# Latent attention rebuilt with four heads side by side, inside a three-block transformer kernel

## The chip, the core and the metric

The program runs on one core of a Trainium2 chip. A core has five engines that run their own in-order streams of instructions and wait for one another through semaphores: PE (matrix multiplication), ACT, DVE, POOL and SP (which here only issues DMAs). The metric is the device time of one execution in microseconds, the median of several runs; lower is better. The profile comes from one execution of its own.

## The reference, cut to what matters

256 tokens of width 1024 go through three blocks: a mixer with a feed-forward net, latent attention with a feed-forward net, and a chunked attention with a gated net. All is float32. Only the latent attention in the middle is touched:

```python
C_HEADS, C_NOPE, C_ROPE, C_V, Q_LORA, KV_LORA = 16, 64, 32, 64, 384, 256

def mla_mixer(h, positions, w_in, q_g, kv_g, w_uq, w_ukv, w_out):
    cq, ckv, kr = jnp.split(h @ w_in, [Q_LORA, Q_LORA + KV_LORA], axis=-1)
    q = (rms_norm(cq, q_g) @ w_uq).reshape(bsz, seq, C_HEADS, C_NOPE + C_ROPE)
    kv = (rms_norm(ckv, kv_g) @ w_ukv).reshape(bsz, seq, C_HEADS, C_NOPE + C_V)
    ...
    q_rope = apply_rope(q[..., C_NOPE:], cos, sin)
    k_rope = apply_rope(kr[:, :, None, :], cos, sin)
    qf = jnp.concatenate([q[..., :C_NOPE], q_rope], axis=-1)
    kf = jnp.concatenate([kv[..., :C_NOPE], jnp.broadcast_to(k_rope, ...)], axis=-1)
    v = kv[..., C_NOPE:]
    ...
        s = jnp.einsum("bqhd,bkhd->bhqk", qblk, kf) * scale
        pr = jax.nn.softmax(s, axis=-1)
        return jnp.einsum("bhqk,bkhd->bqhd", pr, v)
    ...
    return o @ w_out
```

A head's score is thus a product over 96 numbers: 64 of its own ("nope") and 32 rotated ones ("rope"), whose key is the same for all 16 heads.

## The kernel before

Everything is kept feature by feature: a tile holds 128 features on its partitions and the 256 tokens along its rows. A weight matrix comes in chunks of 1 MB. `Stream` handles them: SP loads a chunk into `raw`, ACT rounds it to `whi`, and DVE (or POOL, for the chunks listed in `ON_POOL`) makes the rest `wlo = raw - whi`. `Stream.done()` puts these pieces into a list of due times (`later`), and each group of matmuls advances the clock of that list by `later.tick`. A chunk's splitting can begin when one of four pairs `whi`, `wlo` is free, that is when PE has finished with an older chunk. A product in nearly full precision takes three matmuls, `three`: high by high, high by low, low by high. In this document such a group of three, 256 columns each, is called a triple. Plain float32 matmuls (scores, transposes, values by probabilities) take two passes each in the trace, so one of them shows as two.

The stage of latent attention goes in this order. `tgemm` with `c_evac` makes the five latent tiles (40 triples), in the order keys first (2 tiles), queries (3 tiles), four of them side by side. `rkv_chain` and `rq_chain` work out the norms of the latents; `kv_split` multiplies the latent keys by their norm and only then splits them into `ch` and `cl`. `thin` makes the shared rotated key, which SP copies into all heads by a DMA (line 989). `uq_evac` and `uk_evac` bring queries and keys into `qT` and `kT`, 96 partitions by head, after 36 and 16 triples. Then the values, 24 matmuls of 512 columns (lines 1086 to 1088).

`attend(i)` runs the 16 heads one after another: `sc` the scores (line 1028), a maximum on DVE (1032), two exponentials on ACT (1035), `nrm` the division on DVE (1043), `tr` four transposes (1050) and a copy (1052), `pv` the product with the values (1062). The scores go to the PSUM pool `mm`, four banks; transposes and products go to `aux`, four banks too. The output projection (`tgemm` with `residual`, 64 triples) takes four tiles side by side, then the others in twos, with the last heads mixed in. The order of PE's instructions is chosen by a scheduler in this stage, as is that of the other engines. The feed-forward net follows at once: its first triples need `x` block by block.

## Time and profile before

| | us |
|---|---|
| median of 3 runs | 912.94 |
| lowest, highest | 912.53, 916.38 |
| the profiled execution, its own time | 918.1 |
| its span, first to last instruction | 916.4 |
| PE busy in the span | 889.9 (97%) |
| DVE, ACT, POOL busy | 583.3, 481.3, 268.0 |

The profiled execution lies 5.2 us above the median, so what is worked out from it is used as a difference and put on the median. PE is busy almost all the time: only work taken from PE, or one of its few waits, can shorten the whole. "Busy" counts a matmul that streams at half the clock as fully busy, so the granted clock has to be read beside it.

### The profile page before, as it was taken

The page shows a single profiled execution, that of the slowest core. Times are in us where ns is not written, and L with a number is a line of the kernel's source. Part 1 is how long each engine was busy: PE and PEld are TensorE (multiplying, and loading weights), DVE is VectorE, ACT ScalarE, POOL GpSimd, SP SyncE. Part 2 cuts the span into 40 slices and gives each one's busy share as a digit, 9 for nine tenths or more (in the row PEclk, how much of TensorE's full clock was granted, in tenths as well). Part 3 has the DMA queues.
Part 4 walks back from the last instruction along what each step waited for, and adds up shares of the span by engine and source line. Part 5 has one row for each costly group of instructions (what it writes and reads, how often), then busy time and mean ns, then how long its engine had stood idle before and what let it go on. Part 6 is the DMA issues. An engine that isn't in the chain of part 4 may idle for free.

```text
span 916.4 us, 16411 instructions
## 1 busy us (share of the span) xinstructions
PE 889.9 (97%) x6680; PEld 824.1 (90%) x6680; DVE 583.3 (64%) x943; ACT 481.3 (53%) x848; POOL 268.0 (29%) x269
## 2 busy tenths in 40 slices
PE   7899999999999998999999999999999999999997
PEld 5788999999999987679999999999967789999885
DVE  7697889555555379846755555547783766666442
ACT  6675467555444275756555544424376665544331
POOL 5876733333011266047333301110147000000000
PEclk9999999999999998999999999999999999999999
DMA  8543454655554336014565555549432465555521
GB/s 293 199 150 126 142 187 161 230 189 191 188 191 164 109 116 230 1 57 150 207 211 189 191 187 191 185 164 248 189 138 93 174 246 191 194 185 189 189 82 46
DMA packets 26107, 154.90 MB, mean 169 GB/s; under 512 B 2752, under 2 KB 5744, under 8 KB 8752
## 3 DMA queue, kind: packets, MB, share of 16 engines
q1 hardware_dynamic: 22704, 148.70, 45.6%
q10 hardware_dynamic: 3040, 4.36, 1.9%
q8 instruction: 52, 0.85, 0.4%
q0 software_dynamic: 288, 0.79, 0.3%
q14 instruction: 23, 0.19, 0.1%
HBM read 152.25 MB, written 1.07 MB: 167 GB/s over the span
## 4 chain that ended last, share of the span: by engine, by line
PE 58%; DVE 1%; issue 0%; ACT 0%; DVEq 0%; POOLq 0%; ACTq 0%
PE mm L368 12%; PE mm L369 12%; PE mm L370 12%; PE aux L466 2%; PE aux L465 2%; PE aux L467 2%; PE mm L1028 2%; PE aux L1062 2%; PE mm L430 2%; PE mm L432 2%; PE mm L431 2%; PE aux L1050 1%; PE mm L465 1%; PE mm L467 1%; PE mm L466 1%; PE aux L1219 1%
## 5 line engine op out<-in xcount | busy, mean ns | idle before, releaser
L149 ACT ACTIVATE whi<-raw 128x1024 fp32r<-128x1024 f32 (+3 forms) x318 | 284.9, 949 | 240.2 <-PE mm L369 157.0
L152 DVE TENSOR_TENSOR wlo<-raw,whi 128x1024 fp32r<-128x1024 f32 (+2 forms) x254 | 307.5, 1246 | 124.4 <-ACT whi L149 122.7
L368 PE MATMUL mm<-xh,whi 128*128 128x256 f32 x1072 | 301.4, 281 | 0.8 <-DVE head L494 0.8
L369 PE MATMUL mm<-xl,whi 128*128 128x256 f32 x1072 | 299.1, 279 | 0.0
L370 PE MATMUL mm<-xh,wlo 128*128 128x256 f32 x1072 | 299.0, 279 | 0.0
L370 PEld LDWEIGHTS mm<-xh,wlo 128*128 128x128 f32 x1072 | 203.9, 190 | 0.0
L368 PEld LDWEIGHTS mm<-xh,whi 128*128 128x128 f32 x1072 | 202.0, 188 | 1.7 <-DVE head L494 1.0
L369 PEld LDWEIGHTS mm<-xl,whi 128*128 128x128 f32 x1072 | 202.0, 188 | 0.2
L368 PE MATMUL mm<-hh,whi 128*128 128x256 f32 x512 | 143.9, 281 | 0.0
L369 PE MATMUL mm<-hl,whi 128*128 128x256 f32 x512 | 143.9, 281 | 0.0
L370 PE MATMUL mm<-hh,wlo 128*128 128x256 f32 x512 | 143.9, 281 | 0.0
L152 POOL TENSOR_TENSOR wlo<-raw,whi 128x512 fp32r<-128x512 f32 (+2 forms) x64 | 84.5, 1349 | 67.0 <-ACT whi L149 66.9
L370 PEld LDWEIGHTS mm<-hh,wlo 128*128 128x128 f32 x512 | 98.3, 192 | 0.0
L368 PEld LDWEIGHTS mm<-hh,whi 128*128 128x128 f32 x512 | 96.1, 188 | 0.0
L369 PEld LDWEIGHTS mm<-hl,whi 128*128 128x128 f32 x512 | 96.1, 188 | 0.0
L519 POOL TENSOR_TENSOR fu<-ft 128x512 f32<-128x512 f32 (+1 forms) x36 | 54.7, 1521 | 119.3 <-ACT ft L517 111.6
L313 POOL TENSOR_TENSOR s_acc<-s_acc,sq 128x256 f32<-128x256 f32 x37 | 43.9, 1193 | 155.2 <-ACT sq L312 144.6
L1120 POOL TENSOR_TENSOR r<-v,nhalf 128x1 f32<-128x1 f32 x4 | 2.2, 557 | 193.5 <-DVE v L1119 193.5
L430 PE MATMUL mm<-whi,xh 128*128 128x512 f32 x96 | 39.1, 424 | 1.9 <-ACT whi L149 1.9
L431 PE MATMUL mm<-wlo,xh 128*128 128x512 f32 x96 | 38.1, 400 | 2.2 <-DVE wlo L152 2.2
L520 DVE TENSOR_TENSOR hl<-fu,hh 128x512 fp32r<-128x512 f32 (+1 forms) x36 | 24.1, 675 | 23.4 <-POOL fu L519 23.4
L432 PE MATMUL mm<-whi,xl 128*128 128x512 f32 x96 | 37.9, 398 | 0.6 <-DVE xl L1329 0.6
(370 smaller groups left out, 1355.7 us busy)
## 6 DMA issues: line engine op xcount, KB each, us to landing
raw<-in_w_dram SPq DMA_DIRECT2D x64, 1024.0 KB, 4.8
raw<-in_w_gu_dram SPq DMA_DIRECT2D x22, 1024.0 KB, 4.8
raw<-in_w_qk_dram SPq DMA_DIRECT2D x12, 1024.0 KB, 6.1
raw<-in_w_down_dram SPq DMA_DIRECT2D x11, 1024.0 KB, 4.8
raw<-in_w_ab_out_dram SPq DMA_DIRECT2D x4, 1024.0 KB, 4.9
raw<-in_w_c_out_dram SPq DMA_DIRECT2D x4, 1024.0 KB, 4.8
raw<-in_w_v_dram SPq DMA_DIRECT2D x4, 1024.0 KB, 6.1
raw<-in_w_o_dram SPq DMA_DIRECT2D x4, 1024.0 KB, 4.9
```

Of the source, the lines that this page charges most:

```text
L149: self.nc.scalar.activation(hi[:, s], r[:, s], AF.Copy)
L152: eng.tensor_tensor(lo[:, s], r[:, s], hi[:, s].bitcast(F32), op=ALU.subtract)
L313: state["sum"] = (dve if k == last else pool).tensor_tensor(acc, acc, sq, op=ALU.add)
L368: pe.matmul(ps, wh, h, start=start, stop=False)
L369: pe.matmul(ps, wh, l, start=False, stop=False)
L370: pe.matmul(ps, wl, h, start=False, stop=stop)
L430: pe.matmul(pss[tt], h[k][:, ts], wh[:, s], start=k == 0, stop=False)
L431: pe.matmul(pss[tt], h[k][:, ts], wl[:, s], start=False, stop=False)
L432: pe.matmul(pss[tt], l[k][:, ts], wh[:, s], start=False, stop=k == nk - 1)
L465: pe.matmul(ps, h[k][:, ts], wh[:, ns], start=k == 0, stop=False)
L466: pe.matmul(ps, h[k][:, ts], wl[:, ns], start=False, stop=False)
L519: pool.tensor_tensor(u[:, 0:g], t[:, 0:g], t[:, 0:g], op=ALU.mult)
```

## The change

- The 16 heads are taken in four groups of four. The nope part of a score uses 64 rows of the PE array, two heads at a time on the two halves of the partitions. The rope part uses 32 rows, four heads at a time on the four quarters; it adds to the same PSUM banks. `qn`, `kn`, `qr` and `kr` hold these parts as the projections leave them, so the copies into 96 partitions by head are gone, and with them the DMA of the rotated key; `fold4` writes it to the four quarters.
- A pair's two products with the values (`pv`) alternate, each on 64 columns of the array.
- The latent keys are no longer multiplied by their norm before the split. `k_nope` and `values` apply it as they take their results from PSUM; `kv_split` goes.
- PE's order is now written out by hand over the whole stage (`manual_schedule`): the two latent tiles of the keys first, then the queries; the rope part, then nope queries and keys of one group ahead of the scores.
- The scores of a group take four `aux` banks, all there are; `tr` and `pv` take theirs from the same four.
- Half of the divisions in `nrm` move from DVE to POOL.
- The output projection goes `k` by `k` over all eight tiles in four `mm` banks, with one `pv` and one `tr` within each `k`.

```diff
-              "w_uq", "w_uk", "w_uv", "w_c_out", "w1_1", "w2_1", "w_qk2", "w_v2",
+              "w_uq", "w_uk", "w_uv", "w_uq2", "w_c_out", "w1_1", "w2_1", "w_qk2", "w_v2",
...
+    for i in range(4):
+        pool.tensor_copy(fold4[:, 32 * i:32 * i + 32], fold)
...
-        qT = ap.tile([96, NH, T], F32, name="qT")
-        kT = ap.tile([96, NH, T], F32, name="kT")
+        qn = [ap.tile([P, 2, T], F32, tag="q", name="qn", bufs=4) for _ in range(4)]
+        kn = [ap.tile([P, 2, T], F32, tag="k", name="kn", bufs=4) for _ in range(4)]
+        qr = ap.tile([P, 4, T], F32, name="qr")
+        kr = ap.tile([P, T], F32, name="kr")
         v = ap.tile([P, 2, D], F32, name="v")
-        yh = ap.tile([P, KB, T], F32R, name="yh")
...
-            bcast(rbc[1], rkv, dt=2.0)
-            later(2.1, kv_split)
-        def kv_split():
-            for j in range(2):
-                dve.tensor_tensor(ckv[:, j], ckv[:, j], rbc[1], op=ALU.mult)
-                act.activation(ch[:, j], ckv[:, j], AF.Copy)
-                dve.tensor_tensor(cl[:, j], ckv[:, j], ch[:, j].bitcast(F32), op=ALU.subtract)
+            bcast(rbc[1], rkv, dt=5.5)
...
-        later(3.3, c_chain)
-        tgemm(XH, XL, KB, 5, c_evac, lead=4, psums={4: auxt})
+            bcast(rbc[0], r_col[0], dt=5.0)
...
+        def tiles(w, b0, h, l, nk, n):
+            ps = mmt().rearrange("p (a b) -> p a b", a=2)
+            wh, wl = w
+            for i in range(n):
+                for k in range(nk):
+                    s = slice((b0 + i * nk + k) * P, (b0 + i * nk + k + 1) * P)
+                    three(ps[:, i], wh[:, s], wl[:, s], h[k], l[k], k == 0, k == nk - 1)
+            return ps
...
+        def q_rope(w, g):
+            ps = tiles(w, 6 * g, CK[2:5], CL[2:5], 3, 2)
+            qs = qr[:, 2 * g:2 * g + 2]
+            q2 = mp.tile([P, 2, T], F32, tag="q2", name="q2")
+            act.activation(qs, ps, AF.Copy)
+            for i in range(2):
+                dve.stream_shuffle(q2[:, i], qs[:, i], SHUF)
+                pool.tensor_tensor(qs[:, i], qs[:, i], cosT, op=ALU.mult)
+                dve.tensor_tensor(q2[:, i], q2[:, i], sinT, op=ALU.mult)
+                dve.tensor_tensor(qs[:, i], qs[:, i], q2[:, i], op=ALU.add)
+        def q_nope(w, g):
+            dve.tensor_copy(qn[g], tiles(w, 6 * (g % 2), CK[2:5], CL[2:5], 3, 2))
+        def k_nope(w, g):
+            ps = tiles(w, 4 * g, CK[0:2], CL[0:2], 2, 2)
+            for i in range(2):
+                dve.tensor_tensor(kn[g][:, i], ps[:, i], rbc[1], op=ALU.mult)
+        def values(w, n, tt):
+            ts = slice(tt * P, (tt + 1) * P)
+            ps = mmt()
+            wh, wl = w
+            for k in range(2):
+                s = slice(k * D + n * 512, k * D + n * 512 + 512)
+                pe.matmul(ps, ch[:, k, ts], wh[:, s], start=k == 0, stop=False)
+                pe.matmul(ps, ch[:, k, ts], wl[:, s], start=False, stop=False)
+                pe.matmul(ps, cl[:, k, ts], wh[:, s], start=False, stop=k == 1)
+            later.tick(1.3)
+            act.activation(v[:, tt, n * 512:(n + 1) * 512], ps, AF.Copy, scale=rkv[:, tt:tt + 1])
...
         kr4 = tmp.tile([P, T], F32, tag="rs", name="kr4")
+        mctx = tc.manual_schedule(engines={mybir.EngineType.PE})
+        mctx.__enter__()
+        later(4.2, c_chain)
...
+        w = S.get()
+        q_rope(w, 0)
+        key_rope()
+        q_rope(w, 1)
+        S.done()
+        w = S.get()
+        q_nope(w, 0)
+        wk = S.get()
+        k_nope(wk, 0)
+        q_nope(w, 1)
+        S.done(held=2)
+        k_nope(wk, 1)
+        wv = S.get()
+        values(wv, 0, 0)
...
-        nc.sync.dma_start(kT[64:96], spread(kr.unsqueeze(1), 1, NH))
...
+        def sc(a):
+            pss = [auxt().rearrange("p (a b) -> p a b", a=2) for _ in range(4)]
+            for p in range(2):
+                for qt in range(2):
+                    for i, rr in enumerate(HALF):
+                        pe.matmul(pss[2 * p + i][:, qt], qn[a][rr, p, qt * P:(qt + 1) * P], kn[a][rr, p],
+                                  start=qt == 0, stop=False)
             for qt in range(2):
+                for i in range(4):
+                    rr = slice(32 * i, 32 * i + 32)
+                    pe.matmul(pss[i][:, qt], qr[rr, a, qt * P:(qt + 1) * P], kr[rr], start=False, stop=qt == 1)
+            later.tick(2.6)
+            for p in range(2):
+                mx = mp.tile([P, 2, 2], F32, tag="mx", name="mx", bufs=3)
+                sm = mp.tile([P, 2, 2], F32, tag="sm", name="sm", bufs=8)
+                prs = [mp.tile([P, 2, T], F32, tag="pr", name="pr", bufs=16) for _ in range(2)]
+                for i in range(2):
+                    dve.tensor_reduce(mx[:, i], pss[2 * p + i], axis=AX, op=ALU.max)
+                dve.tensor_tensor(mx, mx, spread(nsrq.unsqueeze(1), 1, 2), op=ALU.mult)
+                for i in range(2):
+                    for qt in range(2):
+                        S.behind = act.activation(prs[i][:, qt], pss[2 * p + i][:, qt], AF.Exp,
+                                                  scale=srq[:, qt:qt + 1], bias=mx[:, i, qt:qt + 1],
+                                                  accum_out=sm[:, i, qt:qt + 1])
+                st_p[2 * a + p] = (prs, sm)
+        def nrm(j):
+            prs, sm = st_p[j]
             dve.reciprocal(sm, sm)
+            for i in range(2):
+                for qt in range(2):
+                    (pool if i else dve).tensor_scalar(prs[i][:, qt], prs[i][:, qt], sm[:, i, qt:qt + 1], None,
+                                                       op0=ALU.mult)
+        def tr(j):
+            prs, sm = st_p.pop(j)
+            st_t[j] = []
+            for i in range(2):
+                ps = auxt().rearrange("p (a b) -> p a b", a=2)
+                for kt in range(2):
+                    for qt in range(2):
+                        pe.transpose(ps[:, kt, qt * P:(qt + 1) * P], prs[i][:, qt, kt * P:(kt + 1) * P], ident)
+                pT = pT_[(2 * j + i) % 3]
+                (act.activation(pT, ps, AF.Copy) if i else dve.tensor_copy(pT, ps))
+                st_t[j].append(pT)
+            later.tick(0.9)
+        def pv(j):
+            pTs = st_t.pop(j)
+            o = auxt()
             for kt in range(2):
+                for i, rr in enumerate(HALF):
+                    pe.matmul(o[rr, 0:T], v[:, kt, (2 * j + i) * 64:(2 * j + i + 1) * 64], pTs[i][:, kt],
+                              start=kt == 0, stop=kt == 1)
+            later.tick(0.9)
+            if j % 2 == 0:
+                state["yh"] = ap.tile([P, 2, T], F32R, tag="q", name="yh", bufs=4)
+                state["yl"] = ap.tile([P, 2, T], F32R, tag="k", name="yl", bufs=4)
+            yh[j], yl[j] = state["yh"][:, j % 2], state["yl"][:, j % 2]
+            S.behind = act.activation(yh[j], o[:, 0:T], AF.Copy)
+            dve.tensor_tensor(yl[j], o[:, 0:T], yh[j].bitcast(F32), op=ALU.subtract)
...
+        sc(0)
+        w = S.get()
+        q_nope(w, 2)
+        k_nope(wk, 2)
+        values(wv, 0, 1)
+        nrm(0)
+        nrm(1)
+        sc(1)
+        q_nope(w, 3)
+        S.done(held=3)
+        k_nope(wk, 3)
+        S.done(held=2)
+        values(wv, 1, 0)
+        nrm(2)
+        nrm(3)
+        sc(2)
+        tr(0)
+        values(wv, 1, 1)
         S.done()
-        for i in range(3, NH):
-            attend(i)
-        tgemm(per_k(yh), per_k(yl), KB, 8, lambda m, ps: residual(m, ps, s_acc[1], "ffn_norm1"), lead=4,
-              pre={0: lambda: attend(16), 1: lambda: attend(17), 3: lambda: attend(18), 5: lambda: attend(19)})
+        nrm(4)
+        nrm(5)
+        pv(0)
+        tr(1)
+        sc(3)
+        nrm(6)
+        nrm(7)
+        pss = [mmt().rearrange("p (a b) -> p a b", a=2) for _ in range(4)]
+        def c_out(w, m, k):
+            wh, wl = w
+            s = slice((k % 2 * KB + m) * P, (k % 2 * KB + m + 1) * P)
+            three(pss[m // 2][:, m % 2], wh[:, s], wl[:, s], yh[k], yl[k], k == 0 and m % 2 == 0,
+                  k == KB - 1 and m % 2 == 1)
+        for k in range(6):
+            if k % 2 == 0:
+                w = S.get()
+            for n in range(2):
+                if n:
+                    (tr(k + 2) if k + 2 < 8 else None)
+                else:
+                    pv(k + 1)
+                for m in range(4 * n, 4 * n + 4):
+                    c_out(w, m, k)
+            if k % 2:
+                S.done()
+        w = S.get()
+        for g in range(4):
+            if g == 0:
+                pv(7)
+            for m in (2 * g, 2 * g + 1):
+                for k in (6, 7):
+                    c_out(w, m, k)
+            hot(residual, 2 * g, pss[g], s_acc[1], "ffn_norm1")
+        S.done()
+        mctx.__exit__(None, None, None)
...
-    o["w_c_out"] = _blocks(i["c_w_out"][0])
+    o["w_c_out"] = _full(i["c_w_out"][0])```

The built programs differ in this stage and in four small copies near the start. Three places show it, in the order in which the instructions stand on an engine, without any time.

PE, in the middle of the attention, before: `kT,qT` are scores of a head, `ident,pr` transposes, `pT,v` products with the values.

```order
L1028 MATMUL mm<-kT,qT 128x256 x10
L1050 MATMUL aux<-ident,pr 128x128
L1028 MATMUL mm<-kT,qT 128x256 x2
L1050 MATMUL aux<-ident,pr 128x128 x3
L1028 MATMUL mm<-kT,qT 128x256 x2
L1050 MATMUL aux<-ident,pr 128x128 x4
L1028 MATMUL mm<-kT,qT 128x256 x2
L1062 MATMUL aux<-pT,v 64x256 x2
```

PE at the same place now, from the scores of the third group on: `kn,qn` and `kr,qr` are the two parts of the scores, `ch`, `cl` with `whi`, `wlo` the last quarter of the values.

```order
L1072 MATMUL aux<-kn,qn 128x256 x8
L1077 MATMUL aux<-kr,qr 128x256 x8
L1108 MATMUL aux<-ident,pr 128x128 x8
L1019 MATMUL mm<-whi,ch 128x512
L1020 MATMUL mm<-wlo,ch 128x512
L1021 MATMUL mm<-whi,cl 128x512
```

Before, the scores of five heads ran ahead and went to other banks than the transposes; now the transposes stand right behind the scores and use the same four banks.

ACT around the beginning of the attention, before: `whi<-raw` is weight splitting, `kT` and `v` copies, `pr,sm` the exponentials.

```order
L149 ACTIVATE whi<-raw 128x1024 x2
L1015 ACTIVATE kT<-mm 64x2x256 x4
L1089 ACTIVATE v<-aux 128x512 x4
L1035 ACTIVATE pr,sm<-mm,mx,srq 128x256 x10
L1052 ACTIVATE pT<-aux 128x512
L1035 ACTIVATE pr,sm<-mm,mx,srq 128x256 x4
```

ACT now, from the exponentials of the first group on:

```order
L1088 ACTIVATE pr,sm<-aux,mx,srq 128x256 x8
L1023 ACTIVATE v<-mm,rkv 128x512
L1088 ACTIVATE pr,sm<-aux,mx,srq 128x256 x8
L149 ACTIVATE whi<-raw 128x1024 x4
L1023 ACTIVATE v<-mm,rkv 128x512
L1088 ACTIVATE pr,sm<-aux,mx,srq 128x256 x8
L149 ACTIVATE whi<-raw 128x512
L1110 ACTIVATE pT_3646<-aux 128x512
```

The four pieces of the first two chunks of the output projection now stand between the exponentials of the second and of the third group.

DVE ahead of the first score maxima, before: `wlo<-raw,whi` is weight splitting, `mx` the maxima.

```order
L152 TENSOR_TENSOR wlo<-raw,whi 128x1024 x2
L1016 COPY kT<-mm 64x2x256 x4
L1032 TENSOR_REDUCE mx<-mm 128x2
L1033 TENSOR_TENSOR mx<-mx,nsrq 128x2
L1032 TENSOR_REDUCE mx<-mm 128x2
```

DVE now, between the divisions of the second group and the maxima of the third:

```order
L1098 TENSOR_SCALAR pr<-pr,sm 128x256 x2
L152 TENSOR_TENSOR wlo<-raw,whi 128x1024 x4
L1084 TENSOR_REDUCE mx<-aux 128x2 x4
L1085 TENSOR_TENSOR mx<-mx,nsrq 128x4 x2
L1095 RECIPROCAL sm<-sm 128x4
L1110 COPY pT_3645<-aux 128x512
```

The same four pieces stand ahead of the maxima of the third group here, and the maxima come four at a time.

## Rows read from the trace of the kernel before

**Rows 1.** Busy time by stretch: PE, PEld, DVE, ACT, POOL; clock; DMA.

```profile
312.69:327.48 14.79, 14.68 (x128) 14.48 (x126) 5.18 (x14) 6.01 (x15) 2.92 (x4) 1.00 0.19 63
327.48:362.35 34.87, 28.98 (x209) 25.68 (x209) 33.04 (x52) 22.65 (x41) 27.14 (x26) 0.95 0.52 189
362.35:394.80 32.45, 32.45 (x144) 22.26 (x145) 26.25 (x83) 20.69 (x65) 0.00 (x0) 0.89 0.09 33
394.80:428.23 33.43, 32.96 (x243) 28.14 (x242) 13.84 (x29) 19.35 (x43) 21.15 (x16) 1.00 0.28 95
```

**Rows 2.** PE's waits over the whole span, longest first.

```profile
PE mm L1028 <- DVE kT L1016: 2.8, 1, 2.8
PE aux L1087 <- POOL wlo L152: 2.6, 1, 2.6
```

**Rows 3.** Busy time by stretch, columns as above, at half clock.

```profile
345.29:348.71 3.42, 3.42 (x18) 3.31 (x17) 3.42 (x3) 1.02 (x2) 3.42 (x2) 0.50 0.43 180
...
362.36:369.19 6.83, 6.83 (x16) 5.49 (x17) 4.78 (x12) 2.73 (x9) 0.00 (x0) 0.50 0.42 155
```

**Rows 4.** Timeline of PE: start, duration, line, shapes; one head's round.

```profile
372.74 1.03 PE L1028 MATMUL mm<-kT,qT 96*128 96x256 f32 x4
373.70 1.08 PE L1062 MATMUL aux<-pT,v 128*64 128x256 f32 x4
374.71 0.66 PE L1050 MATMUL aux<-ident,pr 128*128 128x128 f32 x4
375.20 1.03 PE L1028 MATMUL mm<-kT,qT 96*128 96x256 f32 x4
```

**Rows 5.** Timeline of PE: ten triples, then values, five matmuls from first to last.

```profile
317.73 0.28 PE L368 MATMUL mm<-xh,whi 128*128 128x256 f32 x1
...
321.14 0.28 PE L368 MATMUL mm<-xh,whi 128*128 128x256 f32 x1
...
350.46 0.39 PE L1086 MATMUL aux<-whi,ch 128*128 128x512 f32 x1
...
351.60 0.39 PE L1088 MATMUL aux<-whi,cl 128*128 128x512 f32 x1
```

**Rows 6.** PE on parts of the array elsewhere: timeline, and the forms of L1219.

```profile
328.53 1.07 PE L363 MATMUL aux<-head,ws 128*32 128x256 f32 x16
...
657.48 0.93 PE L1219 MATMUL aux<-kT,qT 64*128 64x128 f32 x8
...
675.85 0.87 PE L1269 MATMUL aux<-pT,v 128*64 128x256 f32 x8
...
L1219 PE MATMUL aux<-kT,qT x64: 272/374/378, 657.5 to 690.3; 64*128 64x128 f32 x32, 64*128 64x256 f32 x32
```

**Rows 7.** Timeline of DVE: one maximum and the instruction behind it.

```profile
373.52 0.68 DVE L1032 TENSOR_REDUCE mx<-mm 128x2 f32<-128x512 f32 x1
374.12 0.15 DVE L1041 RECIPROCAL sm<-sm 128x2 f32<-128x2 f32 x1
```

**Rows 8.** Timeline of ACT: two exponentials, then two weight pieces of 1024 columns.

```profile
365.65 0.56 ACT L1035 ACTIVATE pr<-mm,mx,srq 128x256 f32<-128x256 f32 x1 [5.50 <-DVE mx L1033]
...
366.21 0.55 ACT L1035 ACTIVATE pr<-mm,mx,srq 128x256 f32<-128x256 f32 x1
...
353.00 2.01 ACT L149 ACTIVATE whi<-raw 128x1024 fp32r<-128x1024 f32 x2 [2.08 <-DMA raw<-in_w_c_out_dram]
```

**Rows 9.** Timelines of DVE and POOL: weight pieces, first with POOL at work.

```profile
343.70 4.39 DVE L152 TENSOR_TENSOR wlo<-raw,whi 128x1024 fp32r<-128x1024 f32 x2
...
359.21 2.36 DVE L152 TENSOR_TENSOR wlo<-raw,whi 128x1024 fp32r<-128x1024 f32 x2
...
400.23 10.09 POOL L152 TENSOR_TENSOR wlo<-raw,whi 128x512 fp32r<-128x512 f32 x8 [41.76 <-ACT whi L149]
```

**Rows 10.** Timelines: PE early in the next net, POOL near the program's start.

```profile
432.53 0.39 PE L368 MATMUL mm<-xh,whi 128*128 128x256 f32 x1 [0.84 <-DVE head L494]
...
6.92 0.73 POOL L313 TENSOR_TENSOR s_acc<-s_acc,sq 128x256 f32<-128x256 f32 x1 [3.21 <-ACT sq L312]
```

More of the change, by code (lines that the diff above doesn't have):

```diff
@@ L30 @@
 PAD_X = 1216 // 4
-PAD_W = 4800 // 4
+PAD_W = 4800 // 4 - P
 WARM_UP = 8
@@ L235, in block_kernel @@
     fold = gap.tile([P, 32], F32, name="fold")
+    fold4 = gap.tile([P, P], F32, name="fold4")
     cosT = gap.tile([P, T], F32, name="cosT")
@@ L964, in c_evac @@
                 if j == 1:
-                    later(2.0, rkv_chain)
+                    later(4.4, rkv_chain)
                 if j == 4:
-                    later(3.5, rq_chain)
+                    later(6.0, rq_chain)
         def c_chain():
@@ L971, in c_chain @@
             dve.tensor_tensor(r2, r_col[0], r_col[0], op=ALU.mult)
-            bcast(rbc[0], r_col[0], dt=2.5)
-        later(3.3, c_chain)
-        tgemm(XH, XL, KB, 5, c_evac, lead=4, psums={4: auxt})
-        kr4 = tmp.tile([P, T], F32, tag="rs", name="kr4")
-        act.activation(kr4, thin(wkr, "c_norm"), AF.Copy)
-        pk = auxt()
-        pe.matmul(pk[0:32, 0:T], fold, kr4, start=True, stop=True)
-        SHUF = [(i + 16) % 32 for i in range(32)]
-        kr = mp.tile([32, T], F32, tag="kr", name="kr", bufs=1)
@@ L1010, in block_kernel, with key_rope @@
-        tgemm(per_k(ch, 5)[2:5], per_k(cl, 5)[2:5], 3, 12, uq_evac, bpc=12)
-        def uk_evac(m, ps):
-            h = 2 * m
-            k4 = kT[0:64, h:h + 4].rearrange("p (a b) t -> p a b t", b=2)
-            act.activation(k4[:, :, 0], ps[0:64], AF.Copy)
-            dve.tensor_copy(k4[:, :, 1], ps[64:128])
-        tgemm(per_k(ch, 5)[0:2], per_k(cl, 5)[0:2], 2, 8, uk_evac)
+            bcast(rbc[0], r_col[0], dt=5.0)
+        SHUF = [(i + 16) % 32 for i in range(32)]
+        def key_rope():
+            pk = auxt()
+            pe.matmul(pk[:, 0:T], fold4, kr4, start=True, stop=True)
+            k2 = mp.tile([P, T], F32, tag="k2", name="k2", bufs=1)
+            dve.tensor_tensor(kr, pk[:, 0:T], rbc[0], op=ALU.mult)
+            dve.stream_shuffle(k2, kr, SHUF)
+            pool.tensor_tensor(kr, kr, cosT, op=ALU.mult)
+            dve.tensor_tensor(k2, k2, sinT, op=ALU.mult)
+            dve.tensor_tensor(kr, kr, k2, op=ALU.add)
@@ new lines, in block_kernel @@
+        kr4 = tmp.tile([P, T], F32, tag="rs", name="kr4")
+        mctx = tc.manual_schedule(engines={mybir.EngineType.PE})
+        mctx.__enter__()
+        later(4.2, c_chain)
+        w = S.get()
+        pss = [mmt()[:, 0:T] for _ in range(2)]
+        for k in range(KB):
+            for i in range(2):
+                s = slice((i * KB + k) * P, (i * KB + k + 1) * P)
+                three(pss[i], w[0][:, s], w[1][:, s], XH[k], XL[k], k == 0, k == KB - 1)
+        for i in range(2):
+            hot(c_evac, i, pss[i].unsqueeze(1))
@@ L1023, in block_kernel @@
         st_p, st_t = {}, {}
-        def sc(h):
-            ps = mmt().rearrange("p (a b) -> p a b", a=2)
-            for qt in range(2):
-                pe.matmul(ps[:, qt], qT[:, h, qt * P:(qt + 1) * P], kT[:, h], start=True, stop=True)
-            mx = mp.tile([P, 2], F32, tag="mx", name="mx", bufs=3)
-            sm = mp.tile([P, 2], F32, tag="sm", name="sm", bufs=4)
-            pr = mp.tile([P, 2, T], F32, tag="pr", name="pr", bufs=4)
-            dve.tensor_reduce(mx, ps, axis=AX, op=ALU.max)
-            dve.tensor_tensor(mx, mx, nsrq, op=ALU.mult)
-            for qt in range(2):
-                S.behind = act.activation(pr[:, qt], ps[:, qt], AF.Exp, scale=srq[:, qt:qt + 1],
-                                          bias=mx[:, qt:qt + 1], accum_out=sm[:, qt:qt + 1])
-            st_p[h] = (pr, sm)
@@ L1055, in pv @@
-        def pv(h):
-            pT = st_t.pop(h)
-            if h % 2 == 0:
-                state["o"] = auxt()
-            o = state["o"]
-            rr = slice(64 * (h % 2), 64 * (h % 2) + 64)
-            for kt in range(2):
-                pe.matmul(o[rr, 0:T], v[:, kt, h * 64:(h + 1) * 64], pT[:, kt], start=kt == 0, stop=kt == 1)
-            if h % 2:
-                j = h // 2
-                act.activation(yh[:, j], o[:, 0:T], AF.Copy)
-                dve.tensor_tensor(yl[:, j], o[:, 0:T], yh[:, j].bitcast(F32), op=ALU.subtract)
@@ new lines, in nrm @@
+        def nrm(j):
+            prs, sm = st_p[j]
+            dve.reciprocal(sm, sm)
+            for i in range(2):
+                for qt in range(2):
[4 more added lines that the diff above has]
+            st_t[j] = []
+            for i in range(2):
+                ps = auxt().rearrange("p (a b) -> p a b", a=2)
[6 more added lines that the diff above has]
+            later.tick(0.9)
@@ new lines, in c_out @@
+        def c_out(w, m, k):
[14 more added lines that the diff above has]
+            if k % 2:
+                S.done()
```

83 lines of the change are left out of this document (16 added, 67 removed).

## The prediction

> **What bounds the kernel now.** I read the shares of busy time first: PE is busy 97% of the span, so only PE's work, its waits and its clock count. Then the busy time by stretch over the stage that changes [rows 1]. The four stretches are the latent tiles, the other projections, the attention, and the output projection with the last heads. They add up to 14.8 + 34.9 + 32.5 + 33.4 = 115.5 us, from the first latent triple to the first triple of the feed-forward net. The reader is to see where PE is not busy: 5.9 of the second stretch. The list of waits names it [rows 2]: 2.8 for the last key copies on DVE and 2.6 for a weight piece on POOL. The granted clock is to be read next [rows 3]. PE came back at half of its 2.4 GHz after both waits, for 3.4 and 6.8 us, and did in them what takes half as long at full clock: 1.7 and 3.4 us more. So waits of 5.4 us cost 10.5. In the attention PE itself is the bound: no idle time, against 26.3 of DVE and 20.7 of ACT in 32.5 us [rows 1].
>
> **PE's work after the change.** A plain float32 pass of 256 columns takes 0.217 us: four of them in a head's scores leave 0.96 from start to start with the change-over, and a head's round is 375.20 - 372.74 = 2.46 [rows 4]. Of it the scores are 0.96, the product with the values 1.01, the transposes 0.49. Sixteen rounds are 39.4 us.
>
> The new scores of four heads have 16 nope passes, two at a time, and 16 rope passes, four at a time. Two at a time on halves of the rows is shown: line 1219 has eight passes, half of 128 columns and half of 256, in a slot of 0.86 (next start 658.34), where one after another they would take 4 x 0.217 + 4 x 0.11 = 1.3 [rows 6]. Four at a time is shown for quarters of the columns (16 passes in 1.0, line 363), and not for quarters of the rows. So the rope passes take 0.87 or, one by one, 3.5. I take 0.87, since the pair on row halves and the four on column quarters both run together. A group's scores are then 1.74 + 0.87 = 2.6, for four heads that took 3.84. A pair's `pv` becomes 0.87 for 2.02, as the eight mixed passes of line 1269 in 0.80 show [rows 6]. Transposes stay.
>
> A triple takes (321.14 - 317.73) / 10 = 0.341, a values matmul (351.60 - 350.46) / 5 = 0.228 [rows 5]. Triples and values stay as many as they were. Change-overs between kinds of matmul cost about 0.1 each, an estimate from the 0.14 between `pv` and transposes [rows 4], and there are more of them: I charge 0.3 for each block set among triples.
>
> If PE had only to work, the stage would be: up to the end of the first scores 72 triples (24.6), six values (1.4), statistics, thin product and rope key (2.9), scores (2.6), eight change-overs (2.0), 33.5 together. Two more groups with ten triples, six values and scores each, 3.4 + 1.4 + 2.6 + 0.6 = 8.0, twice. Then `tr`, values, `pv`, `tr` and the last scores with change-overs, 8.0. Then 64 triples (21.8), seven `pv` (6.1), six `tr` (5.9), 13 blocks at 0.3 (3.9), 37.7. The sum is 95.2, 20.3 below now.
>
> **The waits after the change.** The scores of a group take all four `aux` banks, and the order gives PE nothing that could start before banks come free. So the chain from bank to bank counts:
> - Four maxima at 0.60 [rows 7], two small products at 0.15, hand-overs about 0.5 in all: 3.2. Then eight exponentials at 0.56 = 4.5 [rows 8]. The next group's second pair and its rope part can run only behind the last of them, 1.75. From the end of one group's scores to the end of the next that is 9.5, where PE has 8.0 of work. Two such rounds, 19.0.
> - Behind the third scores stand the transposes, on the same banks. Ahead of its exponentials ACT has four weight pieces of 1.0 [rows 8], and DVE the last of them, 1.2 [rows 9], then the maxima, 2.8. The first bank comes free two exponentials later, 1.1. With hand-overs 9.6 behind the exponentials of the second group, which end 1.9 before the third scores do: PE idle for 7.7.
> - Then ACT again: six exponentials (3.4), a weight piece and a copy (1.05), `pv`; values copy, `yh`, three weight pieces, a copy (3.0); then 1.75 of scores, hand-overs 0.8: 10.0 from the first transpose to the end of the last scores.
> - `pv(1)` waits for a bank of the last scores: maxima 2.8, two exponentials 1.1, hand-over 0.3, idle 4.2.
> - The last part has its 37.7, and 1.7 for half clock, if PE comes back from that wait as at 345.29 [rows 3].
>
> The first part: the query latents are split on DVE behind a key weight piece, and the rope queries wait for them some 0.5. So 34.0 + 19.0 + 7.7 + 10.0 + 4.2 + 39.4 = 114.3.
>
> DVE and POOL slow each other: two pieces of 1024 columns took 4.39 beside POOL's and 2.36 alone, 1.0 more for one [rows 9]. Ahead of the first maxima DVE has three such stretches of weight or rope work with POOL at work on its own, and one ahead of the third. So 0 to 4 us; I take 1.5, since part of it falls under PE's projections. Sum 115.8, 0.3 above now.
>
> The Trainium skill, TensorEngine Tiling (Array Packing), section PSUM Bottleneck, speaks against this change: tiling the array speeds up matmuls but not the emptying of PSUM, which may then bound. By the rows of now, where PE alone bounds the attention [rows 1], the sum would be 95.2; by that rule it is the 115.8 above, and the trace cannot show it yet, since nothing waits for a bank there. The same page, section Theoretical Speedup, has up to 4x for 32 rows: by it the rope passes take the 0.87 that I chose.
>
> **Edits at nothing.** `kv_split` goes with its work on DVE and ACT; nothing takes its place but the scaling in `kn` and `values`. The rope key's DMA and the 32-row adds go. `qn` and `kn` come from PSUM by DVE, about 2 us per group, under projections; without that cover the next scores would start as much later. `fold4` costs four small copies on POOL, which idles 3.2 us there [rows 10]. Divisions on POOL lie under the next group's scores. The net behind the stage waits 0.84 for `x` as it does now [rows 10], since `x` is again made in twos at the end.
>
> **The rivals.**
> - *The chain hides*: banks come free as fast as PE wants them. For: in the present attention DVE is idle for 6.2 and ACT for 11.8 of 32.5 us [rows 1]. Against: the order of ACT and DVE. Stage 95.2, time 892.6. Chance 0.10.
> - *Half of it*: the four weight pieces are through before the third scores end, since ACT is early. For: ACT has 12 us of idle time in the second stretch [rows 1]. Against: they stand behind the second group's exponentials. The idle 7.7 goes, time 905.5. Chance 0.14.
> - *Slower, by the clock*: PE falls to 1.2 GHz behind the 1.5 us of waiting in each group too and stays there as long as at 362.36 [rows 3]. Scores behind the bank then take 3.5 instead of 1.75 in three groups (5.3), and the last part loses 1.7 more: time 920. For: both waits of now did it. Against: the 0.84 wait did not [rows 10]. It decides if more than some 12 us of the stage are at half clock. Chance 0.19.
> - *Slower, by the rope passes*: quarters of rows one after another, 2.6 in each group, 10.4 in all, 923.6. Against: rows 6. Chance 0.08.
>
> **Numbers.** The forecast, chance 0.49, is 912.94 + 0.3 = 913.2, in its own range of 911.7 (no slowing on DVE) to 915.7 (all 4 us). Half a per cent, 4.6 us, is about what a measurement of this kernel can tell from no change. The first two rivals are faster by more, 0.24; the last two slower, 0.27; the forecast is the same, 0.49. The range leaves out the first rival and most of the last: 904 to 921. The profiled execution stood 0.6% above the median; only differences of it are used.
>
> **What the profile would show.** The scores of a group in 2.6 us or in over 4. PE idle for 7 to 9 us ahead of the first transposes, released by an exponential, and for about 4 ahead of the second `pv`. Group to group 9 to 10 us. The first scores ending 33 to 36 us behind the first latent triple, the last part 38 to 40. Half clock behind the two long waits alone. No wait for keys or for POOL's values piece. I am wrong if banks come free earlier, or if PE waits at places that I took as covered: rope queries, the first maxima's `nsrq`, or weights of the output projection on POOL.

## The result and the profile after the change

The changed kernel takes 920.32 us (median of 6 runs, 918.01 to 922.73), beside 914.62 for the one before, timed with it (912.53 to 916.38). The ratio is 1.0064, 95% interval [1.0042, 1.0086]: slower by 0.6%, where I had forecast no change. The time lies inside my range of 904 to 921, near its upper end, and above the forecast's own range of 911.7 to 915.7. Its profiled execution took 922.73 us with a span of 921.0, against 918.1 and 916.4.

The busy time by stretch, as in [rows 1]: PE, PEld, DVE, ACT, POOL, the clock, the DMA. The stretches are the latent tiles, the rope queries' wait, the projections with the first scores, two more rounds, the wait ahead of the first transposes, the middle with the fourth scores and the next wait, and the last part:

```profile
313.40:329.86 16.46, 16.46 (x149) 15.54 (x147) 9.73 (x20) 7.59 (x17) 6.00 (x7) 1.00 0.33 122
329.86:332.15 2.29, 0.00 (x0) 0.00 (x0) 2.29 (x6) 0.42 (x2) 0.10 (x1) 1.00 0.40 131
332.15:352.55 20.40, 20.14 (x141) 18.15 (x141) 15.21 (x33) 8.03 (x15) 13.98 (x12) 0.83 0.47 172
352.55:371.40 18.85, 18.05 (x140) 13.93 (x136) 13.41 (x35) 11.80 (x36) 8.26 (x10) 1.00 0.02 8
371.40:378.82 7.42, 0.00 (x0) 0.03 (x1) 6.15 (x9) 3.40 (x8) 1.80 (x1) 0.64 0.71 264
378.82:393.31 14.49, 10.55 (x62) 7.14 (x62) 6.16 (x15) 8.55 (x25) 8.90 (x8) 0.83 0.21 75
393.31:431.24 37.93, 37.85 (x296) 32.74 (x297) 12.89 (x25) 19.69 (x46) 20.33 (x17) 0.96 0.17 59
```

They add up to 117.8 us; before it was 115.5 [rows 1]. PE is busy for 103.1 of it and has three stretches without work. PE's waits in and just behind the stage, to be set beside [rows 2]:

```profile
PE aux L1108 <- ACT pr L1088: 7.4, 1, 7.4
PE aux L1120 <- ACT pr L1088: 3.9, 1, 3.9
...
PE mm L372 <- DVE cl L949: 2.3, 1, 2.3
PE mm L372 <- DVE xl L303: 1.8, 2, 1.4
...
PE aux L1072 <- ACT pr L1088: 0.8, 2, 0.4
```

The two long waits are for banks of the scores, released by exponentials. The third is that of the rope queries for the low parts of the query latents, which I had put at 0.5. The line of `xl` stands behind the stage, in the next net. The stretches at half clock, to be set beside [rows 3]:

```profile
332.51:339.34 6.83, 6.57 (x28) 6.00 (x27) 1.70 (x3) 4.38 (x11) 2.88 (x4) 0.50 0.13 51
373.47:383.71 10.24, 4.88 (x16) 3.51 (x18) 6.54 (x15) 5.63 (x20) 3.36 (x4) 0.50 0.55 205
393.95:397.36 3.41, 3.41 (x18) 2.72 (x13) 1.77 (x6) 2.87 (x11) 2.49 (x3) 0.50 0.02 5
```

PE was busy for 14.9 us of these 20.5, with work that takes half as long at 2.4 GHz: 7.4 us, where I had 1.7. They stand behind the three long waits. In the two rounds, with waits of 0.4, the clock is 1.00.

The scores of four heads, in PE's timeline (start, duration, line, shapes):

```profile
349.55 2.00 PE L1072 MATMUL aux<-kn,qn 64*128 64x256 f32 x16
351.48 1.15 PE L1077 MATMUL aux<-kr,qr 32*128 32x256 f32 x16
352.55 0.39 PE L371 MATMUL mm<-ch,whi 128*128 128x256 f32 x1
```

From start to next start the 16 rope passes take 1.07, so four at a time do run together on quarters of the rows, and the 16 nope passes 1.93; 3.0 us a group in place of my 2.6.

Why the query latents come late is seen on DVE, and beside it on POOL:

```profile
325.03 0.16 DVE L928 TENSOR_TENSOR lr<-aux,r 128x2 f32<-128x2 f32 x1 [3.65 <-PE aux L922]
325.22 1.02 DVE L929 TENSOR_SCALAR lr<-lr 128x2 f32<-128x2 f32 x1
327.06 0.97 DVE L931 TENSOR_TENSOR rkv<-lr,r_col 128x2 f32<-128x2 f32 x1 [0.82 <-POOL lr L930]
328.07 1.97 DVE L338 TENSOR_SCALAR dg<-ident,rkv 128x128 fp32r<-128x128 f32 x2
329.96 1.21 DVE L152 TENSOR_TENSOR wlo<-raw,whi 128x1024 fp32r<-128x1024 f32 x1
...
331.63 0.86 DVE L949 SCALAR_TENSOR_TENSOR cl<-mm,head,ch 128x256 fp32r<-128x256 f32 x2
```

```profile
325.21 1.01 POOL L152 TENSOR_TENSOR wlo<-raw,whi 128x384 fp32r<-128x384 f32 x1 [2.53 <-ACT whi L149]
326.32 0.70 POOL L930 TENSOR_TENSOR lr<-lr,nhalf 128x2 f32<-128x2 f32 x1
327.00 2.96 POOL L152 TENSOR_TENSOR wlo<-raw,whi 128x384 fp32r<-128x384 f32 x3
```

The chain of the key norm runs ahead of `cl` on DVE. Two operations on 2 columns take about 1.0 us each, and each ends with the POOL weight piece beside it (1.01). The next two, on 128 columns, take 1.97 together and end 0.1 us behind POOL's three pieces (330.04 and 329.96). The operation just before POOL's first piece, at 325.03, took 0.16. So in these rows POOL's work sets how long DVE's small operations take; e3 below puts that to the test.

### The profile page after: what moved, and what is told of

Same layout as the page of the kernel before. It is cut to its first block, busy times and chain, and to the rows that moved or that the text cites. A ratio compares the mean times of both kernels' runs of the same rounds, so it can differ in the third digit from the quotient of the medians.

```text
span 921.0 us, 16496 instructions
## 1 busy us (share of the span) xinstructions
PE 886.4 (96%) x6744; PEld 823.4 (89%) x6744; DVE 571.5 (62%) x913; ACT 473.5 (51%) x832; POOL 274.8 (30%) x281
## 3 DMA queue, kind: packets, MB, share of 16 engines
HBM read 152.25 MB, written 1.07 MB: 166 GB/s over the span
## 4 chain that ended last, share of the span: by engine, by line
PE 82%; DVE 10%; ACT 2%; issue 2%; DMA 1%; POOL 1%; SPq 0%; DVEq 0%; POOLq 0%; ACTq 0%
PE mm L371 20%; PE mm L372 20%; PE mm L373 20%; DVE wlo L152 3%; PE aux L470 2%; PE aux L469 2%; PE aux L468 2%; DVE acc L715 2%; PE mm L433 2%; PE mm L435 2%; PE mm L434 2%; ACT pr L1088 1%; DMA raw<-in_w_qk_dram 1%; DVE mx L1084 1%; PE aux L1120 1%
## 5 line engine op out<-in xcount | busy, mean ns | idle before, releaser
L149 ACT ACTIVATE whi<-raw 128x1024 fp32r<-128x1024 f32 (+3 forms) x318 | 285.2, 949 | 239.6 <-PE mm L372 151.8
L152 DVE TENSOR_TENSOR wlo<-raw,whi 128x1024 fp32r<-128x1024 f32 (+2 forms) x254 | 303.7, 1232 | 121.3 <-ACT whi L149 119.7
L372 PE MATMUL mm<-xl,whi 128*128 128x256 f32 x1080 | 301.9, 280 | 1.8 <-DVE xl L303 1.8
L371 PE MATMUL mm<-xh,whi 128*128 128x256 f32 x1080 | 302.2, 282 | 0.0
L372 PEld LDWEIGHTS mm<-xl,whi 128*128 128x128 f32 x1080 | 204.4, 189 | 2.4 <-DVE xl L303 2.2
L373 PEld LDWEIGHTS mm<-xh,wlo 128*128 128x128 f32 x1080 | 206.4, 191 | 0.0
L371 PEld LDWEIGHTS mm<-xh,whi 128*128 128x128 f32 x1080 | 203.2, 189 | 1.1 <-issue 0.8
L371 PE MATMUL mm<-hh,whi 128*128 128x256 f32 x512 | 143.9, 281 | 0.0
L372 PE MATMUL mm<-hl,whi 128*128 128x256 f32 x512 | 143.9, 281 | 0.0
L372 PEld LDWEIGHTS mm<-hl,whi 128*128 128x128 f32 x512 | 96.1, 188 | 0.0
L371 PEld LDWEIGHTS mm<-hh,whi 128*128 128x128 f32 x512 | 96.1, 188 | 0.0
L152 POOL TENSOR_TENSOR wlo<-raw,whi 128x512 fp32r<-128x512 f32 (+2 forms) x64 | 85.2, 1355 | 35.0 <-ACT whi L149 34.9
L433 PE MATMUL mm<-whi,xh 128*128 128x512 f32 x96 | 39.2, 425 | 0.4 <-ACT whi L149 0.4
L435 PE MATMUL mm<-whi,xl 128*128 128x512 f32 x96 | 37.9, 398 | 0.6 <-DVE xl L1420 0.6
```

What stands on the lines that cost most here:

```text
L149: self.nc.scalar.activation(hi[:, s], r[:, s], AF.Copy)
L152: eng.tensor_tensor(lo[:, s], r[:, s], hi[:, s].bitcast(F32), op=ALU.subtract)
L371: pe.matmul(ps, wh, h, start=start, stop=False)
L372: pe.matmul(ps, wh, l, start=False, stop=False)
L373: pe.matmul(ps, wl, h, start=False, stop=stop)
L433: pe.matmul(pss[tt], h[k][:, ts], wh[:, s], start=k == 0, stop=False)
```

## The experiments

All ten in one table, cut at the same instructions: from the first latent triple to the end of the first scores, two rounds, from the end of the third scores to that of the fourth, and from there to the next net. These four are the stage; "behind" is the rest of the span. The last columns are the median and its ratio to the kernel before, timed beside it.

| kernel | first part | two rounds | 3rd to 4th scores | to the next net | stage | behind | median | ratio |
|---|---|---|---|---|---|---|---|---|
| changed | 39.2 | 18.8 | 18.0 | 41.9 | 117.8 | 489.8 | 920.3 | 1.0064 |
| e1_latents_first | 38.1 | 19.1 | 18.1 | 42.0 | 117.2 | 489.7 | 920.8 | 1.0061 |
| e2_fill | 36.9 | 19.1 | 18.2 | 41.0 | 115.2 | 489.5 | 918.5 | 1.0029 |
| e3_no_pool_piece | 34.2 | 19.5 | 17.5 | 41.9 | 113.1 | 489.6 | 916.6 | 1.0013 |
| e4_other_banks | 38.8 | 18.9 | 13.5 | 43.7 | 114.9 | 489.8 | 917.4 | 1.0027 |
| e5_latents_first_2 | 36.7 | 19.3 | 17.6 | 42.0 | 115.6 | 489.4 | 918.7 | 1.0032 |
| e6_chunk_earlier | 38.3 | 19.9 | 15.9 | 41.9 | 116.0 | 489.6 | 919.4 | 1.0043 |
| e7_three_edits | 34.2 | 20.5 | 10.3 | 43.0 | 108.0 | 487.0 | 908.7 | 0.9928 |
| e8_middle_reordered | 34.2 | 20.5 | 18.4 | 35.9 | 109.0 | 487.0 | 909.0 | 0.9933 |
| e9_inputs_first | 38.3 | 19.5 | 18.4 | 41.9 | 117.9 | 487.0 | 917.7 | 1.0025 |
| e10_second_wait | 34.2 | 20.5 | 10.3 | 40.0 | 105.0 | 487.5 | 906.0 | 0.9904 |

Where the code is the same (changed, e4, e6, e9) the first part spreads from 38.3 to 39.2, so up to about 1 us of a stage's difference can come from there. The kernel before had a median of 914.6 beside the changed kernel and 915.4 to 915.9 beside the experiments; so what an edit saves comes out up to 1.4 us larger by the ratios than by the medians that are compared below. All edits are made on the changed kernel.

**e1_latents_first.**

```
-            bcast(rbc[1], rkv, dt=5.5)
+            bcast(rbc[1], rkv, dt=4.5)
...
-                act.activation(ch[:, j], ps[:, i], AF.Copy, scale=g)
+                e = act.activation(ch[:, j], ps[:, i], AF.Copy, scale=g)
+                S.behind = e if j == 4 else S.behind
...
-                    later(4.4, rkv_chain)
+                    later(9.2, rkv_chain)
```

> Edit: the key norm's chain starts 4.8 later and the key weight pieces stand behind the last query latent, so that on DVE the query latents come first. Theory 'one wait, then the clock': the 2.3 us wait of the rope queries goes, and with it the 6.8 us at half clock behind it; the first scores end 33 to 35 us behind the first latent triple instead of 39.1, everything after keeps its length, time 914 to 915.5. Rival 'DVE is late anyway': the same work is only put off, the keys or the first scores wait for it instead, the first scores end at 37 to 39, time 918 to 921.

The wait for the query latents is gone, but PE waits a little later for the diagonals of the key norm:

```profile
PE aux L345 <- DVE dg L339: 1.7, 1, 1.7
PE aux L345 <- DVE dg L338: 0.9, 1, 0.9
```

That is 2.6 in place of 2.3, and the time is that of the rival. The experiment doesn't tell "DVE is late" from "the edit put the spreading matmul too early".

**e5_latents_first_2.** The same, with that matmul later:

```
-            bcast(rbc[1], rkv, dt=4.5)
+            bcast(rbc[1], rkv, dt=6.4)
```

> Edit: as in the first experiment (query latents ahead of the key norm's chain and of the key weight pieces on DVE), and the matmul that spreads the key norm stands seven triples later on PE, where the first experiment had put it too early and waited 2.6 us for it. Theory 'order': once both are in a fit place, DVE has time enough, no wait over 0.5 is left ahead of the first scores, they end at 34 to 35, time 915 to 917. Rival 'DVE is late anyway': with POOL beside it DVE can't do this work in time in any order, the wait moves on to the keys, the rope part or the first scores, which end at 37 to 38.5, time 919 to 921.

The first part is 36.7 and the ratio 1.0032 [1.0019, 1.0044], between the two theories. PE's waits are down to 0.6, 0.6 and 0.3, but there are still three, and the clock still falls (the last number but two in each line):

```profile
335.00:340.00 5.00, 3.83 (x26) 3.42 (x25) 5.00 (x16) 1.09 (x3) 3.73 (x6) 0.86 0.60 210
340.00:345.00 5.00, 5.00 (x33) 4.82 (x33) 5.00 (x8) 1.79 (x3) 4.15 (x4) 0.80 0.01 3
```

The order is a part of the cause, not the whole.

**e3_no_pool_piece.**

```
-            "w_cin": (2,), "w_uq": (1,), "w_uv": (0,), "w_c_out": (2, 3),
+            "w_cin": (2,), "w_uv": (0,), "w_c_out": (2, 3),
```

> Edit: the weight chunk of 4 x 384 columns that POOL subtracts while DVE makes the key norm's chain is subtracted on DVE, in 2 x 768. DVE gets more to do, POOL nothing in that stretch. Theory 'DVE is held up by POOL': the chain's small operations of 1.0 us take 0.1 to 0.3 each without POOL beside them, that is 3 us or more less for two pieces at about 1.0 each; the rope queries wait under 1.0 instead of 2.3, and the time falls by 2 to 5 to 915 to 918. Rival 'DVE has too much in a row': the small operations stay at 1.0, the two pieces come on top, the wait grows to 4, time 922 to 924.

DVE's timeline at the same place:

```profile
321.14 0.17 DVE L929 TENSOR_SCALAR lr<-lr 128x2 f32<-128x2 f32 x1
321.41 0.99 DVE L152 TENSOR_TENSOR wlo<-raw,whi 128x768 fp32r<-128x768 f32 x1
322.32 0.15 DVE L931 TENSOR_TENSOR rkv<-lr,r_col 128x2 f32<-128x2 f32 x1
322.39 0.94 DVE L152 TENSOR_TENSOR wlo<-raw,whi 128x768 fp32r<-128x768 f32 x1
323.26 0.47 DVE L338 TENSOR_SCALAR dg<-ident,rkv 128x128 fp32r<-128x128 f32 x2
```

The small operations take 0.17, 0.15 and 0.47 where they took 1.02, 0.97 and 1.97. DVE does 1.9 us of pieces more and is through earlier. The wait of 2.3 is gone with the half clock behind it, and the first part is 34.2: 5.0 less than in the changed kernel, 4.0 less than in the fastest of those with the same first part. The time falls by 3.7. One line in the list of POOL's chunks settles most of what went wrong in the first part.

**e2_fill.**

```
+        def fill(n):
+            ps = mmt()
+            for i in range(n):
+                pe.matmul(ps[:, 0:T], ident, cosT, start=i == 0, stop=i == n - 1)
...
+        fill(5)
         w = S.get()
         q_rope(w, 0)
...
+        fill(16)
         tr(0)
...
+        fill(8)
         pss = [mmt().rearrange("p (a b) -> p a b", a=2) for _ in range(4)]
```

> Edit: products that nobody reads are put on PE into the three long waits (5 in the 2.3 us one, 16 in the 7.4, 8 in the 3.9); extra work, the results are as before. The waits themselves stay. Theory 'one wait, then the clock': PE keeps 2.4 GHz behind each wait, which gives back 3.4 us behind the first, 2.4 behind the second and 1.7 behind the third, 7.5 together, time 913 to 915. Rival 'the waits alone': what PE does behind the waits is set by ACT and DVE, not by its clock, gain under 2 us, time 918.5 to 921.

Behind all three waits the clock is now full. Two of the stretches:

```profile
374.10:384.90 10.80, 8.43 (x63) 5.77 (x63) 3.65 (x9) 7.16 (x20) 8.92 (x8) 1.00 0.04 15
388.80:425.80 37.00, 36.42 (x296) 31.64 (x297) 12.95 (x25) 19.86 (x46) 20.50 (x17) 1.00 0.17 60
```

The stage falls by 2.7 and the time by 1.8, not by 7.5: 2.3 in the first part, nothing in the middle, 0.9 at the end. That is what the rival said. In the middle PE at full speed only waits more, for the transposes' copies and for banks. So of the 7.4 us that half clock cost PE about a third is time, or less, since up to 1 us of the 2.3 can be the spread of the first part.

**e4_other_banks.**

```
-        tr(0)
+        tr(0, mmt)
...
-        pv(0)
-        tr(1)
+        pv(0, mmt)
+        tr(1, mmt)
```

> Edit: the transposes and the product with the values that stand between the third and the fourth scores take banks of the projections' pool, not of the scores'. Theory 'the chain from bank to bank': the 7.4 us wait ahead of the first transposes goes, since they no longer wait for an exponential; the fourth scores still wait for the third group's exponentials, so that 1 to 5 us of it come back there. The stage is shorter by 3 to 7, time 913.5 to 917.5. Rival 'ACT and DVE are the limit there, not the banks': the whole wait comes back ahead of the fourth scores, time 919 to 921.

(`tr` and `pv` now take the pool of banks as an argument.) The transposes start at once, and PE's waits move on:

```profile
PE aux L1120 <- ACT pr L1088: 4.4, 1, 4.4
PE mm L1120 <- DVE mx L1085: 4.4, 1, 4.4
```

The second line is the first product with the values: it needs the transposes copied out, and on DVE the copy is queued behind four weight pieces and the maxima:

```profile
367.01 4.82 DVE L152 TENSOR_TENSOR wlo<-raw,whi 128x1024 fp32r<-128x1024 f32 x4
371.75 2.47 DVE L1084 TENSOR_REDUCE mx<-aux 128x2 f32<-128x512 f32 x4
...
374.21 0.68 DVE L1110 COPY pT<-mm 128x512 f32<-128x512 f32 x1
```

From third to fourth scores 4.5 us are saved, and 1.8 come back behind them; with 0.4 of the first part, where nothing was edited, the stage is 3.0 shorter, and so is the time. The bank was one link of the chain, the order of DVE the next.

**e6_chunk_earlier.**

```
         w = S.get()
+        S.done(held=3)
         q_nope(w, 2)
...
         q_nope(w, 3)
-        S.done(held=3)
```

> Edit: the first of the two weight chunks of the output projection is split one round earlier, behind the first group's exponentials, so that two pieces instead of four stand ahead of the third maxima. Theory 'pieces': the 7.4 us wait ahead of the first transposes falls by the two pieces, 2.4 on DVE, to 5.0, and the earlier round grows by at most 0.5, since ACT and DVE wait there for the next scores anyway; time 917.5 to 919. Rival 'as long in either place': the second round grows by 2 or more, time 919.5 to 921.

The wait falls from 7.4 to 5.0, as expected of two pieces, but the round before grows by 1.0, between the theory's 0.5 and the rival's 2. The stage is 1.9 less, of which 1.0 is in the first part, where the code is the same; what the edit itself gives is about 0.9. The ratio is 1.0043 [1.0029, 1.0057], which alone can't be told from the changed kernel's.

**e9_inputs_first.**

```
-        act.activation(xh[:, k], src, AF.Copy, scale=scale)
+        state["xh"] = act.activation(xh[:, k], src, AF.Copy, scale=scale)
...
             hot(residual, 2 * g, pss[g], s_acc[1], "ffn_norm1")
+        S.behind = state["xh"]
         S.done()
```

> Edit: only the fourth edit of the three-edit kernel, on the changed kernel as it is: the weight pieces that follow the stage stand behind the next net's eight inputs on ACT. Theory: the part behind the stage, 489.8 us in the changed kernel and 488.2 in the one before, falls to 487 as it did there, since the waits of 1.4 and 0.4 for the inputs' low parts go; time 917 to 918. Rival: the part behind the stage was shorter in that kernel because of the other edits, here it stays over 489; time 919.5 to 921.

Behind the stage the changed kernel lost 1.4 us, in PE's timeline:

```profile
431.24 0.39 PE L371 MATMUL mm<-xh,whi 128*128 128x256 f32 x2
433.01 0.39 PE L372 MATMUL mm<-xl,whi 128*128 128x256 f32 x1 [1.37 <-DVE xl L303]
```

since on DVE two weight pieces come between the sums `head` and the low part `xl` of the next net's inputs:

```profile
428.16 1.68 DVE L152 TENSOR_TENSOR wlo<-raw,whi 128x1024 fp32r<-128x1024 f32 x1
429.76 0.74 DVE L497 TENSOR_TENSOR head<-mm,head 128x256 f32<-128x256 f32 x2
430.43 1.65 DVE L152 TENSOR_TENSOR wlo<-raw,whi 128x1024 fp32r<-128x1024 f32 x1
432.00 0.95 DVE L303 SCALAR_TENSOR_TENSOR xl<-head,xh 128x256 fp32r<-128x256 f32 x1
```

On ACT the first of the high parts `xh` stands behind weight pieces too (five, from 425.51 to 429.07); the edit moves what follows on both engines, and doesn't tell their shares apart. With the pieces behind the inputs there is no wait, and the rest of the span takes 487.0 instead of 489.8, with the stage as it was. That is more than the 1.8 us of idle time in the list of waits: from start to start of PE's matmuls the same places lost 2.4. The time fell by 2.6.

**e7_three_edits.** The edits of e3, e4, e6 and e9 together.

> Edit: no POOL piece beside the key norm's chain, the projections' banks for the middle transposes and products, the first output chunk a round earlier, and, new, the weight pieces of the net behind the stage stand behind its eight inputs on ACT. Theory: each takes out its own wait: 4.8 + 3.0 + 2.4 in the stage, and 0.8 to 1.2 of the 1.8 us wait behind it, sum 11 to 11.4, stage 107 to 108, time 908.5 to 910.5. Rival 'one chain': the middle part's length is set by ACT's exponentials whichever wait is removed, so that the second and the third don't add, sum 8 to 9, time 911 to 912.5.

The stage is 108.0 and the ratio 0.9928 [0.9909, 0.9946]. The edits add up: 9.9 us off the stage, where they took 4.8, 3.0 and 1.9 one by one, and 2.7 behind it, as e9 did. That is what separate links would give, and not the rival's one chain. Left are these waits:

```profile
PE aux L1120 <- ACT pr L1088: 4.2, 1, 4.2
PE mm L1120 <- DVE mx L1085: 1.9, 1, 1.9
```

**e8_middle_reordered.** On top of e7, the order of PE in the middle:

```
-        sc(2)
         tr(0, mmt)
+        sc(2)
         values(wv, 1, 1)
...
         tr(1, mmt)
+        pv(1, mmt)
+        tr(2, mmt)
         sc(3)
...
-                if n:
+                if k and n:
                     (tr(k + 2) if k + 2 < 8 else None)
-                else:
+                elif k:
                     pv(k + 1)
```

> Edit: as the three edits, and on PE the first transposes stand ahead of the third scores, and the second product with the values and the third transposes ahead of the fourth scores instead of behind them, so that PE has 3 to 4 us more to do while ACT makes exponentials. Theory 'PE only lacks work in front of the banks': 3 to 5 more are saved than with the three edits alone, of the waits ahead of the first product and of the second, stage 103 to 105, time 905 to 907. Rival 'ACT and DVE are full there': the copies of the transposes push the exponentials back by as much, under 1 saved, time as with the three edits.

The rival was right. The products wait for the transposes' copies, which are queued behind maxima and exponentials:

```profile
PE mm L1120 <- DVE pT L1110: 4.8, 1, 4.8
PE mm L1120 <- ACT pT L1110: 2.2, 1, 2.2
```

The last part is 7 us shorter and the middle 8 us longer; the product and the transposes that moved are a part of both.

**e10_second_wait.** On top of e7, the first eight triples of the output projection ahead of the second product:

```
-                if n:
+                if k < 2:
+                    if k:
+                        pv(n + 1)
+                        tr(n + 2)
+                elif n:
                     (tr(k + 2) if k + 2 < 8 else None)
```

> Edit: as the three-edit kernel, and the first eight triples of the output projection stand ahead of the second product with the values instead of around it, so that PE has 2.7 us of work while it waits 4.2 for a bank of the last scores. Theory 'only work is lacking': the wait falls to 1.5 and PE stays at 2.4 GHz behind it, 2.7 to 4.4 less, stage 103.5 to 105.3, time 904 to 906. Rival 'it comes back': the second and third transposes' copies are as late as before, PE waits for them by as much later on, under 1 saved, time 908 to 909.5.

Between the fourth scores and the second product PE now idles for 1.3 of 4.3 us, and the clock stays full in that stretch and in the one behind it:

```profile
374.43:378.72 4.29, 2.94 (x25) 2.74 (x26) 4.15 (x6) 2.41 (x8) 4.29 (x5) 1.00 0.02 4
378.72:414.42 35.70, 34.36 (x273) 28.85 (x274) 12.17 (x26) 18.50 (x45) 21.42 (x19) 1.00 0.28 92
```

At 906.0, ratio 0.9904 [0.9882, 0.9926], it beats the kernel before and the changed one. Against e7 the stage is 3.0 shorter; the ratios' intervals of the two overlap. The triples found all that they need ready there, while the products of e8 waited for copies on DVE and ACT.

## Why the prediction was right or wrong, step by step

The range of 904 to 921 held, but only near its end, and the forecast itself, 913.2, was 7.1 too low. Of this 1.7 is the kernel before, which I had at 912.94 and which measured 914.62 over six runs; the rest is the change of 5.7 where I had forecast 0.3.

**The step that failed** is "The first part: the query latents are split on DVE behind a key weight piece, and the rope queries wait for them some 0.5", which gave 34.0 in my sum. It measured 39.2. The mechanism was there, its size was not: the wait is 2.3, and PE came back from it at half clock for 6.8 us, 3.3 more. e3 takes both out and leaves 34.2. The size was lost in another term, "DVE and POOL slow each other", which I took as 1.5 out of 0 to 4: I had priced it as a longer time for pieces of 1024 columns ahead of the maxima, from [rows 9]. But the key norm's chain of small operations lay beside POOL's pieces, and each took as long as the piece. The order on DVE is a part of it too: e5 changed that alone and took 1.6 to 2.6 us out of the first part.

**The second, smaller one** is "the net behind the stage waits 0.84 for `x` as it does now". It waits 1.4 and 0.4, the low part of `x` being queued behind weight pieces, and the rest of the span is 489.8 after 488.2 [rows 1, 10]. e9 takes 2.7 out.

**What held:** the rounds 9.4 and 9.4 (9.5), the idle time ahead of the first transposes 7.4 (7.7), from the first transpose to the end of the last scores 10.6 (10.0), the wait ahead of the second product 3.9 (4.2), the last part 37.9 (39.4). The rope passes run together, no keys and no values piece are waited for. e4 shows that the first long wait is for banks, e6 that weight pieces are a part of it. PE's work is as worked out: 103.05 busy less 7.43 for half clock is 95.6 (95.2). So the main claim stood: by its busy time, PE alone would bring the stage to 95, and 14.8 us of waits and the half clock behind them, from the chain through DVE, ACT and banks, give it back. The rule on emptying PSUM, from the Trainium skill's TensorEngine Tiling (Array Packing), section PSUM Bottleneck, is borne out in direction: its sum was 115.8, the stage is 117.8, and 95.2 was far off. How much of the waits is the emptying itself, and how much the weight pieces queued ahead of it, e4 and e6 tell only in part.

**The sum.** That the stage is only 2.0 over my 115.8 is in part luck: the first part is 5.2 over, the 1.5 that I had added for slowing covers some of it, and the last part, 1.5 under what I had added up, hides as much again. The stage is 2.0 over, and the rest of the span 1.6 over what it was: 3.6 above the forecast change of 0.3, so 3.9. The measured change is 914.62 x 0.0064 = 5.9, with the interval from 3.8 to 7.9, so 3.9 is at its lower end. The other 2 us lie ahead of the stage or in the spread of runs and stay open: between the two profiled executions 0.7 of the difference lies ahead of the stage, and in those of the changed kernel and the experiments, where the code ahead of the stage is the same, the stage begins between 309.3 and 313.4 us.

**The rival by the clock** gave 920, and its bound of 12 us at half clock was passed (20.5). But its mechanism, a fall behind the short waits of each round, is not there, and e2 shows that the clock alone is worth 2 to 3 us at most. That it named the number was luck; the number came from a wait that I had taken as nearly covered.

## What to carry to other kernels

When work on PE is packed tighter, list for each engine the queue ahead of every value that PE will then wait for, and cost it with the other engines' work running beside it; here a single small chain beside POOL's pieces took back 4 to 5 us. Weight pieces put "where an engine idles" are work in a queue: in these runs those that stood behind the inputs of the next work made PE wait for nothing (e9), those ahead of them cost a wait and, in the first part, a half-clock stretch behind it. To fill a wait, use work that needs nothing more of the engines that cause it: triples in e10 gave 3.0 us of the stage, products in e8 nothing.
